# Two attention cores turn two key blocks into one tile, and the order of all instructions is computed with other costs

## The chip, the core and the metric

The kernel runs on one core of a Trainium2 chip. TensorE (PE) multiplies 128x128 blocks into PSUM; VectorE (DVE), ScalarE (ACT) and GpSimd (POOL) do the elementwise work; SyncE (SP) and ACT issue the transfers (DMA). The metric is the time of one execution on the device in microseconds (us), as a median of several.

## The reference

Two layers work on 512 latent tokens and 256 context tokens of width 1024. Each layer normalises and modulates its input, projects it to 4608 columns, runs three groups of attention heads beside a gate, and projects back. Cut to what matters here:

```python
def layer(x, cx, ...):
    hx = rmsnorm(x, norm_w) * (1 + scale[:, None, :]) + shift[:, None, :]
    px = split_cols(hx @ w_in)                       # the same for the context, hc and pc
    ya, yca = global_gqa(...)                        # A: every latent and context key
    yb, ycb = neighbourhood_attn(...)                # B: 8 x 16 window of keys, plus all context keys
    yc_, ycc = window_gqa(...)                       # C: keys within 128 tokens, plus all context keys, a sink
    ux = jnp.concatenate([ya, yb, yc_], axis=-1) * jax.nn.silu(px[9])
    x = x + gate[:, None, :] * (ux @ w_out)
```

`shift`, `scale` and `gate` come from `silu(c) @ ada_w + ada_b`. The context half is computed in the first layer alone. Everything is float32, and the output is the latent stream after a last RMSNorm.

## The kernel before

**Numbers in two parts.** Each operand of a large product is split into a high part (rounded to the matmul's float32r) and a low part, and three products (high-high, high-low, low-high) are added in PSUM. So a weight tile `ws` becomes `wh` (ACT, line 242) and `wl` (DVE or POOL, line 245), and a tile T of PSUM becomes `pth` (ACT) and `ptl` (DVE) in `pt_copy` (line 1019).

**Stages.** `body` first computes the modulation and the normalised, modulated input h. For each of 8 blocks of 128 features it loads two halves of an `ada` block (line 195), multiplies them (line 210), turns the result (line 218) and makes h (lines 394 to 400), from which the first matmuls of the projections (line 416) follow. The sums of squares of the input are added over the partitions by line 347 into `Obig`, raised to the power -1/2 on POOL (line 356), spread by line 364 into `Sbig`, and copied by ACT into `rb` (line 387). `mixers` then weaves the projections of the next head pair (lines 308 and 329) between the attention steps of the present one. The second half of the program's layer, p2, projects back (line 505) and prepares the next layer's h.

**One attention unit.** A unit is one head. `scores` multiplies query blocks with keys into `Sbig` (line 1028), DVE takes the row maximum, ACT the exponential into a tile P in SBUF, with queries on the partitions. The product with the values needs keys on the partitions, so P has to be turned block by block. `ship` (line 1030) has SP copy P into a tile R (`R5`, or `R2` for a smaller part) by DMA from SBUF to SBUF. `values` turns the 128x128 blocks of R for one key block into a PSUM tile T (`turn_r`, line 1042; shown as L1044), `pt_copy` brings T to SBUF, and `pv` multiplies it with the values into `Obig`. There are two tiles T, each one PSUM bank. `BandUnit` is group C, `NearUnit` group B, `GlobalUnit` group A; `CtxUnit` handles the context's queries. Key blocks 4 and 5 are the context, and all four query blocks use them. Of the latent key blocks, in C 0 and 3 are used by two query blocks each and 1 and 2 by three; in B all four are used by two. The loops take one key block per T, so a key block that two query blocks use fills 256 of T's 512 columns.

**What sets the order.** The loops only record instructions. `arrange` then computes the order in which each engine issues them: `Graph.run` goes through them as a list scheduler with costs per instruction, `Graph.back` gives ranks from the end, and the best of six rounds is fixed as the order of each engine. On the chip each engine issues in that order and waits for what an instruction needs; so the costs never become times, they only decide what stands ahead of what. The costs before: a DMA takes 2550 ns plus its bytes at 395 per ns, one after the other over all queues; a matmul that follows turnings costs 86 ns more; after a turning the next choice is a turning into the same tile T, if one is ready.

## Time and profile before

| | |
|---|---|
| median of 3 runs | 1173.37 us (1170.91, 1173.37, 1175.30) |
| the profiled execution, its own time | 1171.95 us |
| its span, first to last instruction | 1170.2 us |
| instructions in the span | 22714 |
| mean granted clock of PE | 0.995 |
| DMA | 191.41 MB, 164 GB/s on average |
| copies of P into R | 216 of 256 KB, 64 of 128 KB, 32 of 64 KB |

The page gives busy time per engine, the chain of work that ended last, and the costliest groups of instructions by line, with their mean duration and with the idle time of the engine ahead of them. Matmuls overlap in PE's pipeline, so their durations (about 0.28 us for 256 columns) are longer than the step from one start to the next; prices of PE's work are therefore read from the starts in the list of instructions in order of time. In that list a piece is: start, length, engine, line, operation, out<-in, shapes, count.

### The profile page before, as it was taken

How to read it: one execution, taken by the hardware profiler on the slowest of the kernel's cores; microseconds unless marked ns; L12 is line 12 of the kernel's file. 1: busy time of each engine (PE TensorE's matmuls, PEld its weight loads, DVE VectorE, ACT ScalarE, POOL GpSimd, SP SyncE). 2: the span in 40 equal slices, each digit the busy share in tenths (PEclk: the TensorE clock that was granted, in tenths of full speed). 3: DMA queues.
4: the chain of work that ended last, by engine and by line, in shares of the span. 5: the costliest groups of instructions: out<-in, count | busy, mean ns of one | idle time of the engine just before them, and what ended most of it. 6: DMA issues, size and time to landing. Idle time of an engine off the chain costs nothing.

```text
span 1170.2 us, 22714 instructions
## 1 busy us (share of the span) xinstructions
PE 1130.1 (97%) x8016; PEld 1015.5 (87%) x8016; DVE 765.4 (65%) x1548; ACT 696.4 (60%) x1581; POOL 406.7 (35%) x496
## 2 busy tenths in 40 slices
PE   5999999999999999999899999999999999999996
PEld 3799999998798897988787999988998989898886
DVE  6657676666456566666879765668674666667653
ACT  5546655565557567677742543555566777778651
POOL 2431212135446346357400021222234575667001
PEclk9999999999999999999999999999999999999999
DMA  9545434425444445435758542554243454556352
GB/s 350 196 131 177 152 123 160 147 102 169 146 154 156 155 149 192 156 131 182 251 188 304 175 138 83 172 176 139 103 160 122 156 169 149 172 180 216 118 172 72
DMA packets 105761, 191.41 MB, mean 164 GB/s; under 512 B 12208, under 2 KB 30768, under 8 KB 105648
## 3 DMA queue, kind: packets, MB, share of 16 engines
q1 hardware_dynamic: 101616, 181.71, 46.5%
q10 hardware_dynamic: 4032, 8.26, 1.9%
q8 instruction: 63, 1.03, 0.4%
q14 instruction: 50, 0.41, 0.1%
HBM read 109.05 MB, written 11.14 MB: 103 GB/s over the span
## 4 chain that ended last, share of the span: by engine, by line
PE 81%; DMA 6%; DVE 6%; ACT 4%; issue 2%; POOL 1%; SPq 0%; DVEq 0%; ACTq 0%; POOLq 0%
PE pj L329 18%; PE pj L308 18%; PE Obig L1028 9%; PE Sbig L1028 9%; PE T L1044 6%; PE pj L505 5%; DMA R<-P 4%; PE T L505 3%; PE Sbig L505 3%; PE T L329 2%; PE Sbig L416 1%; PE T L1047 1%; PE Sbig L329 1%; DVE junk L151 1%; PE pj L416 1%
## 5 line engine op out<-in xcount | busy, mean ns | idle before, releaser
L1024 DVE TENSOR_TENSOR ptl<-T,pth 128x512 fp32r<-128x512 f32 (+2 forms) x312 | 181.9, 592 | 98.4 <-ACT pth L778 93.8
L778 ACT ACTIVATE pth<-T 128x512 fp32r<-128x512 f32 (+2 forms) x312 | 159.2, 521 | 87.5 <-PE T L1044 75.9
L329 PE MATMUL pj<-wh,hL 128*128 128x256 f32 x896 | 184.4, 287 | 0.6 <-DVE kt L906 0.4
L308 PE MATMUL pj<-hL,wh 128*128 128x512 f32 x544 | 183.2, 401 | 0.3 <-DVE qt L894 0.2
L242 ACT ACTIVATE wh<-ws 128x512 fp32r<-128x512 f32 x192 | 120.0, 631 | 86.6 <-PE pj L308 25.1
L1028 PE MATMUL Sbig<-kt,qt 128*128 128x256 f32 (+1 forms) x864 | 155.7, 306 | 0.5 <-ACT P L1119 0.3
L329 PEld LDWEIGHTS pj<-wh,hL 128*128 128x128 f32 x896 | 145.7, 190 | 2.0 <-issue 0.7
L1044 PEld LDWEIGHTS T<-identr,R 128*128 128x128 f32 x1024 | 112.9, 141 | 33.0 <-DMA R<-P 9.4
L245 POOL TENSOR_TENSOR wl<-ws,wh 128x512 fp32r<-128x512 f32 x76 | 98.7, 1306 | 120.2 <-ACT wh L242 102.9
L1044 PE MATMUL T<-identr,R 128*128 128x128 f32 x1024 | 126.7, 239 | 10.2 <-DMA R<-P 6.7
L1028 PEld LDWEIGHTS Sbig<-kt,qt 128*128 128x128 f32 x864 | 125.1, 189 | 9.7 <-ACT P L1119 1.1
L1028 PE MATMUL Obig<-pth,vt 128*128 128x256 f32 (+2 forms) x432 | 128.7, 308 | 0.3 <-ACT pth L778 0.3
L1028 PE MATMUL Obig<-ptl,vt 128*128 128x256 f32 (+2 forms) x432 | 128.6, 312 | 0.2 <-DVE ptl L1024 0.2
L329 PE MATMUL pj<-wl,hL 128*128 128x256 f32 x448 | 128.0, 286 | 0.0
L245 DVE TENSOR_TENSOR wl<-ws,wh 128x512 fp32r<-128x512 f32 x116 | 82.5, 719 | 48.3 <-ACT wh L242 38.0
L308 PEld LDWEIGHTS pj<-hL,wh 128*128 128x128 f32 x544 | 98.3, 189 | 15.7 <-issue 0.4
L308 PE MATMUL pj<-hL,wl 128*128 128x512 f32 x272 | 109.2, 401 | 0.1
L1028 PEld LDWEIGHTS Obig<-pth,vt 128*128 128x128 f32 x432 | 81.4, 188 | 7.0 <-issue 1.5
L1150 DVE TENSOR_REDUCE negm<-Sbig 128x1 f32<-128x768 f32 x64 | 61.1, 955 | 38.4 <-PE Sbig L1028 22.4
L329 PEld LDWEIGHTS pj<-wl,hL 128*128 128x128 f32 x448 | 85.1, 190 | 0.4
L1028 PEld LDWEIGHTS Obig<-ptl,vt 128*128 128x128 f32 x432 | 81.5, 189 | 4.4 <-issue 0.9
L356 POOL TENSOR_TENSOR rstd<-rstd,mhalf 128x2 f32<-128x2 f32 (+1 forms) x6 | 5.4, 902 | 200.6 <-DVE rstd L354 200.6
(336 smaller groups left out, 2535.1 us busy)
## 6 DMA issues: line engine op xcount, KB each, us to landing
R<-P SPq DMA_DIRECT2D x216, 256.0 KB, 2.4
ws<-wf_dram SPq DMA_DIRECT2D x72, 256.0 KB, 3.3
ws<-wt_dram SPq DMA_DIRECT2D x72, 256.0 KB, 3.1
ada<-adaw_dram SPq DMA_DIRECT2D x32, 512.0 KB, 5.6
ws<-wo_dram SPq DMA_DIRECT2D x57, 256.0 KB, 3.4
bm<-mskB_dram SPq DMA_DIRECT2D x16, 576.0 KB, 4.2
R<-P SPq DMA_DIRECT2D x64, 128.0 KB, 2.2
dots<-adat_dram SPq DMA_DIRECT2D x16, 256.0 KB, 3.3
```

The lines of the kernel that those rows point to most:

```text
L151: return nc.vector.tensor_tensor_reduce(out=junk, in0=w, in1=row, op0=OP.mult, op1=OP.add, scale=1.0, scalar=m if half else sm[:, c:c + 1] ...
L242: nc.scalar.activation(hi, src, AF.Copy)
L245: eng.tensor_sub(lo, src, hi.bitcast(F32))
L308: nc.tensor.matmul(p[:, 0:n], a[:, r, :], cols(b[kt], c0, n), start=(i == 0), stop=(i == 23))
L329: nc.tensor.matmul(p[:, t * 256:(t + 1) * 256], tok(a[kt], t2 + t), b[:, r, :], start=(i == 0), stop=(i == 23))
L416: mm = nc.tensor.matmul(out, a, b, start=begin, stop=(kt == KT - 1 and i == 2), skip_group_check=True)
L505: nc.tensor.matmul(p[:, 0:n], a[:, r, :], ucols(ua[b][ft], c0, n), start=(ft == FT_ORDER[0] and i == 0), stop=(ft == FT_ORDER[-1] and i == 2))
L778: nc.scalar.activation(out, src, AF.Copy)
L1024: nc.vector.tensor_sub(lo[:, 0:n], T[:, 0:n], hi[:, 0:n].bitcast(F32))
L1028: return nc.tensor.matmul(*args, **kw)
L1044: return nc.tensor.transpose(out.bitcast(F32R), src, identr)
L1150: nc.vector.tensor_reduce(nm, S, axis=AX.X, op=OP.max, negate=True)
```

## The change

It has two parts. First, `values` of groups C and B puts two small key blocks into one tile T: 0 and 3 in C, 1 with 3 and 2 with 0 in B. The turnings and the products stay as many as they were, of the same widths; 96 copies of 256 columns by `pt_copy` (each by ACT and DVE) become 48 of 512. Which key block begins and which ends the accumulation in `Obig` is now named by its number.

Second, the planner's costs change. A DMA now has a fixed part and a rate by its source: 2400 ns and 340 bytes per ns from DRAM ("far"), 1650 and 395 from SBUF; transfers follow each other per issuing queue, overlap between queues costs half its length, and 700 ns pass to the landing. PE's steps count double before 21 us, a third turning in a row costs 20 ns more, float32 products are priced by shape. And after a turning, when none for the same T is ready, a turning into any tile that can be opened is now taken.

```diff
 class BandUnit(Unit):
         def values(self):
             O = psO()
-            for n, kb in enumerate((4, 5, 0, 1, 2, 3)):
-                qs = [i for i in range(4) if kb in self.pos[i]]
+            for kbs in ((4,), (5,), (0, 3), (1,), (2,)):
                 T = psT()
-                for j, i in enumerate(qs):
+                jobs = [(kb, [i for i in range(4) if kb in self.pos[i]]) for kb in kbs]
+                for j, (kb, i) in enumerate((kb, i) for kb, qs in jobs for i in qs):
                     o = self.pos[i][kb]
                     turn_r(T[:, j * 128:(j + 1) * 128], self.P[i], o)
-                k = len(qs) * 128
+                k = 128 * sum(len(qs) for _, qs in jobs)
                 pt = pt_copy(T, k)
                 yield k / 1200
-                pv(O, self.v(kb), pt, 0, qs[0] * 128, k, n == 0, n == 5)
+                o = 0
+                for kb, qs in jobs:
+                    pv(O, self.v(kb), pt, o, qs[0] * 128, len(qs) * 128, kb == 4, kb == 2)
+                    o += len(qs) * 128
                 yield k / 1200
...
 class NearUnit(Unit):
-            for n, kb in enumerate((4, 5, 1, 2, 3, 0)):
+            for kbs in ((4,), (5,), (1, 3), (2, 0)):
...
-TO_PE, TO_OTHER, FIXED, RATE = 400.0, 150.0, 2550.0, 395.0
+TO_PE, TO_OTHER, TO_LAND = 400.0, 150.0, 700.0
+SLOW = 21000.0
...
-            self.move = 3460.0 if stem(outs[0][0].name) == "bc" else b / RATE
+            far = any(u[0].name not in tiles or tiles[u[0].name][1] for u in ins)
+            self.fixed = 2400.0 if far else 1650.0
+            self.move = 3460.0 if out == "bc" else b / (340.0 if far else 395.0)
...
-            self.busy = (108.0 if n == 128 else 230.0) if exact else n / 2.4 + (13.5 if n > 128 else 12.0)
+            self.busy = {128: 108.0, 256: 57.0, 2: 112.0}[n] if exact else n / 2.4 + (13.5 if n > 128 else 12.0)
...
                 same = [x for x in now[e] if steps[x[1]].turn == prev.turn]
+                if not same:
+                    same = [x for x in now[e] if steps[x[1]].turn and all(
+                        slots[self.tag[z]] and self.place[z] == opened[self.tag[z]] for z in self.opens[x[1]])]
...
-                pipe = fin = max(t + FIXED, pipe) + s.move
+                begin = max(t + s.fixed, ring.get(e, 0.0))
+                fin = begin + s.move
+                for x, (a, b) in data.items():
+                    if x != e:
+                        fin += 0.5 * max(0.0, min(b, fin) - max(a, begin))
+                ring[e], data[e] = fin, (fin - s.move, fin)
                 lanes.append(fin)
+                fin += TO_LAND
...
+                row = row + 1 if s.turn else 0
+                if row > 2 and s.switch > 5:
+                    busy += 20
+                if t < SLOW:
+                    busy *= 2
+                    fin += s.last
```

Such costs move instructions all over the program. Three places matter for what follows.

The beginning of PE's order, before: the sums of squares (L347) stand in three pieces between the products with `ada` (L210).

```order
L347 MATMUL Obig<-ones,sq 128x2 x2
L210 MATMUL T<-ada,silu_c 2x256 x4
L347 MATMUL Obig<-ones,sq 128x2
L210 MATMUL T<-ada,silu_c 2x256 x4
L347 MATMUL Obig<-ones,sq 128x2
L210 MATMUL T<-ada,silu_c 2x256 x4
L218 MATMUL T<-ident,adasb 128x128 x2
L210 MATMUL T<-ada,silu_c 2x256 x4
L139 MATMUL T<-ident,silu_c 128x128 x4
L364 MATMUL Sbig<-ident,rstd 128x128 x4
```

And now:

```order
L347 MATMUL Obig<-ones,sq 128x2 x4
L210 MATMUL T<-ada,silu_c 2x256 x8
L364 MATMUL Sbig<-ident,rstd 128x128 x4
L218 MATMUL T<-ident,adasb 128x128 x2
L210 MATMUL T<-ada,silu_c 2x256 x3
L347 MATMUL Obig<-ones,sq 128x2 x2
L210 MATMUL T<-ada,silu_c 2x256
L139 MATMUL T<-ident,silu_c 128x128 x4
L210 MATMUL T<-ada,silu_c 2x256 x4
L364 MATMUL Sbig<-ident,rstd 128x128 x2
L416 MATMUL pj<-hL,wh 128x512 x2
```

All four sums for the latent tokens stand first, and the spreading of their result (L364) has moved ahead of the turnings L218 and L139.

PE in the first unit of group B that turns all its blocks, before (T and R with their numbers: R5_1608, 1530, 1563 and 1636 are the four query blocks): a matmul stands between the first two key blocks.

```order
L1044 MATMUL T_1638<-identr_77,R5_1608 128x128
L1044 MATMUL T_1638<-identr_77,R5_1530 128x128
L1044 MATMUL T_1638<-identr_77,R5_1563 128x128
L1044 MATMUL T_1638<-identr_77,R5_1636 128x128
L329 MATMUL pj_1707<-wh_1485,hC_625 128x256
L1044 MATMUL T_1683<-identr_77,R5_1608 128x128
L1044 MATMUL T_1683<-identr_77,R5_1530 128x128
L1044 MATMUL T_1683<-identr_77,R5_1563 128x128
L1044 MATMUL T_1683<-identr_77,R5_1636 128x128
```

And now, with the same unit's tiles under new numbers:

```order
L1044 MATMUL T_1618<-identr_77,R5_1588 128x128
L1044 MATMUL T_1618<-identr_77,R5_1510 128x128
L1044 MATMUL T_1618<-identr_77,R5_1543 128x128
L1044 MATMUL T_1618<-identr_77,R5_1616 128x128
L1044 MATMUL T_1663<-identr_77,R5_1588 128x128
L1044 MATMUL T_1663<-identr_77,R5_1510 128x128
L1044 MATMUL T_1663<-identr_77,R5_1543 128x128
L1044 MATMUL T_1663<-identr_77,R5_1616 128x128
L308 MATMUL pj_1792<-hL_241,wl_1783 128x512
```

The eight turnings stand in one row and fill both tiles T.

SP's queue where a unit of group A in the first layer copies its P into R, before:

```order
L251 DMA ws_4791<-wf_dram 128x512
L1039 DMA R5_4071<-P_4069 128x512
L1039 DMA R2_4072<-P_4069 128x256
L195 DMA ada_4057<-adaw_dram 128x1024
L251 DMA ws_4797<-wf_dram 128x512
L195 DMA ada_4059<-adaw_dram 128x1024
L1039 DMA R2_4079<-P_4076 128x256
L1039 DMA R5_4078<-P_4076 128x512
```

And now:

```order
L251 DMA ws_4701<-wf_dram 128x512
L195 DMA ada_3977<-adaw_dram 128x1024
L195 DMA ada_3979<-adaw_dram 128x1024
L251 DMA ws_4707<-wf_dram 128x512
L1039 DMA R5_3991<-P_3989 128x512
L1039 DMA R2_3992<-P_3989 128x256
L1039 DMA R2_3999<-P_3996 128x256
L1039 DMA R5_3998<-P_3996 128x512
```

Both halves of `ada` and the weight have moved ahead of the first pair of copies; before they stood between the two pairs.

More of the change, by code (lines that the diff above doesn't have):

```diff
@@ L1265, in values @@
             O = psO()
-            for n, kb in enumerate((4, 5, 1, 2, 3, 0)):
-                qs = [i for i in range(4) if kb in self.PLAN[i][4]]
+            for kbs in ((4,), (5,), (1, 3), (2, 0)):
                 T = psT()
-                for j, i in enumerate(qs):
+                jobs = [(kb, [i for i in range(4) if kb in self.PLAN[i][4]]) for kb in kbs]
+                for j, (kb, i) in enumerate((kb, i) for kb, qs in jobs for i in qs):
                     o = self.PLAN[i][4][kb]
                     turn_r(T[:, j * 128:(j + 1) * 128], self.P[i], o)
-                k = len(qs) * 128
+                k = 128 * sum(len(qs) for _, qs in jobs)
                 pt = pt_copy(T, k)
                 yield k / 1200
-                out = O[:, qs[0] * 128:qs[0] * 128 + k] if kb else O.rearrange("p (t c) -> p t c", t=4)[:, 0:4:3]
-                pv(out, self.v(kb), pt, 0, None, k, n == 0, n == 5)
+                o = 0
+                for kb, qs in jobs:
+                    n = len(qs) * 128
+                    out = O[:, qs[0] * 128:qs[0] * 128 + n] if kb else O.rearrange("p (t c) -> p t c", t=4)[:, 0:4:3]
+                    pv(out, self.v(kb), pt, o, None, n, kb == 4, kb == 0)
+                    o += n
                 yield k / 1200
@@ L1584, with __init__ @@
 class Step:
-    def __init__(self, inst):
+    def __init__(self, inst, tiles):
         self.inst, self.name = inst, inst.name
@@ L1598, in __init__, with cost @@
                                      str(a.dtype).split(".")[-1]))
-        self.cost()
-    def cost(self):
+        self.cost(tiles)
+    def cost(self, tiles):
         ins = [u for u in self.use if not u[1]]
@@ L1610, in cost @@
             b = 4 * outs[0][2][0][1] * size(outs[0][2])
-            self.busy = ISSUE.get(stem(outs[0][0].name).split("_")[0], 430.0)
-            self.move = 3460.0 if stem(outs[0][0].name) == "bc" else b / RATE
+            out = stem(outs[0][0].name).split("_")[0]
+            far = any(u[0].name not in tiles or tiles[u[0].name][1] for u in ins)
+            self.busy = ISSUE.get(out, 430.0)
+            self.fixed = 2400.0 if far else 1650.0
+            self.move = 3460.0 if out == "bc" else b / (340.0 if far else 395.0)
         elif e == "PE":
@@ L1748, in run @@
                 stage_left[self.pool[t]] += len(v)
-        lanes, pipe = [], 0.0
-        prev, done = None, 0
+        lanes, ring, data = [], {}, {}
+        prev, row, done = None, 0, 0
         def push(k):
@@ L1892, in arrange @@
 def arrange(tc, nc, needed):
-    steps = [Step(i) for i in nc.cur_bb.bb.instructions
+    tiles = {t.name: (t.tag, "DRAM" in str(t.space)) for t in tc.tiles}
+    steps = [Step(i, tiles) for i in nc.cur_bb.bb.instructions
              if type(i).__name__ not in ("BassTilePoolBoundary", "InstRegisterMove")]
-    tiles = {t.name: (t.tag, "DRAM" in str(t.space)) for t in tc.tiles}
     graph = Graph(steps, tiles, needed)
```

## The prediction, as made before the change was run

> **What bounds the kernel now.** I read the page's busy shares first, then the chain of waits, then the busy time by stage.
>
> ```profile
> PE 1130.1 (97%) x8016; PEld 1015.5 (87%) x8016; DVE 765.4 (65%) x1548; ACT 696.4 (60%) x1581; POOL 406.7 (35%) x496
> ...
> PE 81%; DMA 6%; DVE 6%; ACT 4%; issue 2%; POOL 1%; SPq 0%; DVEq 0%; ACTq 0%; POOLq 0%
> ```
>
> TensorE (PE) is busy for 1130.1 of 1170.2 us and holds 81% of the chain that ended last. DVE and ACT have a third of their time free. So the time is the sum of PE's instructions plus 40.1 us in which PE stands still. A change can win in two ways: cheaper PE instructions, or less standing still. Where PE stands still shows in the busy time by stretch (columns: stretch, its length, then busy us and instructions of PE, weight loads, DVE, ACT, POOL, the granted clock, DMA share, GB/s):
>
> ```profile
> 11.33:22.00 10.67, 9.71 (x73) 4.65 (x73) 5.55 (x22) 6.00 (x16) 1.14 (x1) 1.00 1.04 392
> 22.00:50.00 28.00, 26.89 (x215) 20.91 (x213) 19.44 (x46) 15.51 (x37) 13.50 (x11) 1.00 0.84 304
> 50.00:300.00 250.00, 248.69 (x1871) 231.76 (x1871) 165.16 (x354) 143.42 (x348) 67.80 (x94) 1.00 0.42 139
> 300.00:322.00 22.00, 19.67 (x129) 16.41 (x128) 10.52 (x19) 12.20 (x26) 11.39 (x11) 0.92 0.54 167
> 322.00:560.00 238.00, 234.02 (x1773) 209.53 (x1772) 150.04 (x303) 160.12 (x380) 126.09 (x154) 1.00 0.47 160
> 560.00:650.00 90.00, 83.49 (x439) 68.91 (x438) 76.82 (x150) 38.89 (x80) 9.04 (x6) 0.98 0.72 243
> 650.00:1120.00 470.00, 467.10 (x3309) 428.36 (x3308) 310.47 (x607) 296.31 (x661) 172.18 (x208) 1.00 0.45 150
> ```
>
> From 50 to 1120 us PE is idle for 17 us (1.3 + 2.3 + 4.0 + 6.5 + 2.9). The other 23 us are the head, up to 50 us, and the end. What ended the idle time of PE (us in total, times, longest):
>
> ```profile
> PE Obig L347 <- DVE sq L343: 11.3, 1, 11.3
> PE T L1044 <- DMA R<-P: 6.7, 7, 2.3
> PE T L1044 <- DVE ptl L1024: 3.0, 5, 1.8
> ```
>
> In the middle, turnings wait for the copy of P into R (6.7 us) and for a PSUM tile T still being read (3.0 us). A long stand has a second price, read from the granted clock:
>
> ```profile
> 317.90:321.30 3.40, 3.40 (x16) 2.91 (x15) 1.61 (x3) 2.18 (x7) 0.63 (x2) 0.50 0.00 0
> 380.00:384.00 4.00, 2.27 (x18) 1.62 (x18) 1.64 (x4) 1.78 (x6) 3.28 (x3) 1.00 0.87 283
> ...
> 573.90:577.30 3.40, 3.40 (x12) 2.62 (x12) 3.40 (x9) 2.14 (x4) 0.00 (x0) 0.50 0.74 230
> ```
>
> Right after the 2.3 us wait before 317.9 the clock was 0.50 for 3.4 us: 1.7 us of work lost. The same follows at 573.9. The 1.7 us stand within 380 to 384 cost no clock. So a stand over about 2 us costs 1.7 us more. (The Trainium skill, "TensorE: Matmul & The Clock Gate", Part 1, says the clock falls after at least one idle window of about 3.4 us; by that, neither stand should have cost clock and a removed stand would save its own length alone. This trace disagrees, and I go by it.)
>
> **Part 1: turnings in longer rows.** The order of PE's instructions keeps all 1024 turnings of R. Counted over the whole of PE's order, they stood in 315 unbroken rows (84 of two, 28 of three, 176 of four, 8 of five or six, 19 of eight) and now stand in 228 (none of two, 30 of three, 130 of four, 2 of seven, 66 of eight). Price of a row, from PE in order of time:
>
> ```profile
> 117.53 0.46 PE L1044 MATMUL T<-identr,R 128*128 128x128 f32 x4
> 117.83 0.35 PE L329 MATMUL pj<-wl,hL 128*128 128x256 f32 x1
> 118.02 0.40 PE L329 MATMUL pj<-wh,hL 128*128 128x256 f32 x2
> 118.25 0.28 PE L329 MATMUL pj<-wl,hL 128*128 128x256 f32 x1
> ...
> 123.78 0.28 PE L1044 MATMUL T<-identr,R 128*128 128x128 f32 x2
> 123.90 0.35 PE L329 MATMUL pj<-wh,hL 128*128 128x256 f32 x1
> 124.09 0.28 PE L1028 MATMUL Obig<-ptl,vt 128*128 128x256 f32 x1
> ...
> 183.01 0.79 PE L1044 MATMUL T<-identr,R 128*128 128x128 f32 x8
> 183.64 0.35 PE L308 MATMUL pj<-hC,wl 128*128 128x256 f32 x1
> 183.83 0.40 PE L308 MATMUL pj<-hC,wh 128*128 128x256 f32 x2
> ```
>
> Two matmuls of 256 columns step by 0.23 us (118.02 to 118.25), so one is 0.12. From a row's start to the start of the second matmul behind it, less one such step, a row of four costs 118.02 − 117.53 − 0.12 = 0.37, a row of two 124.09 − 123.78 − 0.12 = 0.19, a row of eight 183.83 − 183.01 − 0.12 = 0.70. The matmul behind a row starts its successor 0.07 late (0.19 instead of 0.12), which is what a longer row saves; but turnings from the third on are slower, so two rows of four (0.74) become 0.70 and no more. With three at 0.28 and five, six, seven between (0.45, 0.53, 0.62): before 16.0 + 7.8 + 65.1 + 3.9 + 13.3 = 106.1 us, now 8.4 + 48.1 + 1.2 + 46.2 = 103.9. **Saved: 2.2 us**, all on PE. Bounds: 1 us, if the longest rows run as slowly as four-rows end to end, and 6 us, if each of the 87 rows less saved a whole 0.07.
>
> **Part 2: small key blocks share a tile.** 96 pairs of copies of 256 columns become 48 of 512.
>
> ```profile
> L778 ACT ACTIVATE pth<-T 128x512 fp32r<-128x512 f32 x184 | 107.7, 598 | 49.4 <-PE T L1044 42.0 <-PE Obig L1028 5.4 <-DVE ptl L1024 0.4
> ...
> L778 ACT ACTIVATE pth<-T 128x256 fp32r<-128x256 f32 x96 | 36.7, 384 | 28.6 <-PE T L1044 26.2 <-PE Obig L1028 1.5
> ...
> L1024 DVE TENSOR_TENSOR ptl<-T,pth 128x512 fp32r<-128x512 f32 x184 | 124.9, 687 | 67.6 <-ACT pth L778 64.6 <-PE Obig L1028 1.3
> ```
>
> ACT saves 96 × 0.384 − 48 × 0.598 = 8.2 us, and DVE about as much by the same pairing. Neither sets the end, so this is worth nothing directly; the matmuls into Obig keep number and width. What it can give is earlier-free T tiles. A tile T is free after ACT's 0.60 and DVE's 0.69, 1.3 us, and the hand-overs between the engines; so I count reuses of a T bank that come with under 1.8 us of other PE work since its last turning. In the order before these are 50 of 412, now 23 of 364. (I added up PE's steps, 0.12 for 256 columns and 0.23 for 512, along each order.) Half the short reuses are gone, so I take half of the 3.0 us wait: **1.5 us**; bounds 0 and 3.0.
>
> **Part 3: the beginning.** PE in order of time before:
>
> ```profile
> 11.33 1.02 PE L347 MATMUL Obig<-ones,sq 128*128 128x2 f32 x4 [11.33 <-DVE sq L343]
> ...
> 14.72 0.59 PE L347 MATMUL Obig<-ones,sq 128*128 128x2 f32 x2
> 15.24 1.03 PE L210 MATMUL T<-ada,silu_c 128*2 128x256 f32 x8
> ...
> 15.59 1.14 POOL L356 TENSOR_TENSOR rstd<-rstd,mhalf 128x4 f32<-128x4 f32 x1 [14.30 <-DVE rstd L354]
> ...
> 18.17 0.60 PE L364 MATMUL Sbig<-ident,rstd 128*128 128x128 f32 x4
> ...
> 19.61 0.59 ACT L387 ACTIVATE rb<-Sbig 128x512 f32<-128x512 f32 x1
> ...
> 21.04 0.72 ACT L395 ACTIVATE hL<-x,mod 128x512 fp32r<-128x512 f32 x1 [0.32 <-DVE x L394]
> ...
> 21.97 0.49 PE L416 MATMUL pj<-hL,wh 128*128 128x512 f32 x1
> ```
>
> The sums of squares (L347) stood between groups of L210; now all four stand first, so they end near 13.2 instead of 15.3, the power on POOL near 14.9 instead of 16.7, and L364 follows 8 L210 (two groups, until about 15.2) instead of standing at 18.17. The broadcast `rb` then waits on ACT for the context squares, whose loads SP now issues ahead of the third half of `ada`; I put it near 16.5 instead of 19.61. `hL` would follow at about 18.2 and the first L416 2.9 us earlier. But ahead of it now stand L210, L347, L139 and the second L364, which needs DVE and POOL once more: 18.1 for the first x, 0.3 + 1.14 for the power, so L416 near 20.1. **Saved: 1.8 us**; bounds 0 (the `ada` loads, 392 GB/s at a DMA share of 1.04, set the pace instead) and 2.9. From 22 to 50 us PE is busy 26.89 of 28 us, so the earlier start is carried on and not lost in a wait.
>
> **Part 4: the order of the rest.** SP's queue moves loads against the copies R. Two of the chain's pieces are the late copies, the page's row of issues has the usual one:
>
> ```profile
> 311.05 6.55 DMA R<-P
> ...
> 378.40 5.35 DMA R<-P
> ...
> R<-P SPq DMA_DIRECT2D x216, 256.0 KB, 2.4
> ```
>
> In the first, both halves of an `ada` job and a weight stood ahead of the second pair of copies in SP's queue; now they stand ahead of both pairs (SP's rows in the part on the change). In the second, nothing stood ahead on SP, but ACT had issued a store of `u` just before:
>
> ```profile
> 378.32 0.33 ACTq L1358 DMA_DIRECT2D u<-u  x1
> ```
>
> The new planner counts half of such an overlap between queues; whether it moved this store clear, the order does not tell. Adding up PE's steps between the last score matmul of a block and its first turning: the least is 6.0 us before and 5.7 now, under 8 us 23 copies before and 22 now. So copies are no better covered than they were. I take **1 us** saved (the second place's wait, partly); bounds: 10 saved (all 6.7 and both losses of clock) and 8 lost (two more stands of 2.3 + 1.7).
>
> From the last sums of squares (L633) to the end every engine has the same order as before: nothing.
>
> **The sum** against the profiled execution's own 1171.95 us: − 2.2 − 1.5 − 1.8 − 1.0 = 1165.4 us. The median of the runs, 1173.37, lies 1.4 above that execution and its runs reach from 1170.91 to 1175.3. I put the change at 6.5 us and the time at **1166 us**, between 1165.4 and 1173.4 − 6.5 = 1166.9; own range 1161 to 1171.
>
> **Rivals.** *No change to be told* (about 0.5%, 6 us, is what a measurement of this kernel can tell from no change). Rows and head give 4.0 us, and the waits come back elsewhere, since copies are as tightly covered as before: 1173.4 − 4 + 2 = 1171 us. For it: the unchanged distances in part 4. Against it: fewer short reuses of T.
>
> *More than I say*: both losses of clock go with their stands. Then 6.7 + 3.4 + 3.0 + 2.2 + 1.8 = 17 us: 1156 us. Against it: late copies came from the queue ahead of them, and the queue is as full.
>
> *Slower, by late copies*: at each of the eight late `ada` jobs of the first layer SP now may have both halves ahead of all copies of a unit, as at the first place above. A stand there costs 2.3 + 1.7 = 4.0 us. From two more on, the 6.5 us are gone; with four more: 1173.4 − 6.5 + 16 = 1183 us, with three 1179.
>
> *Slower, by full banks*: a row of eight fills both T tiles, and PE cannot turn again until one is copied. There are 47 more such rows; 0.14 us of waiting at each eats the 6.5 us, 0.35 us gives 1173.4 − 6.5 + 16.5 = 1183 us. Against it: the 19 rows of eight before, as at 183.01, run straight on into matmuls, and reuses with little work between are fewer now. (The Trainium skill, "Perfetto Trace Analysis", section Matmuls, wants independent groups to rotate through PSUM banks so that one is emptied while the next is filled; filling both at once goes against it.)
>
> **How the numbers follow.** Forecast 0.50, no change 0.22, more 0.13, late copies 0.10, full banks 0.05. Against 1173.4, faster by over 0.5% means under 1167.5. I give that 0.8 of the forecast (0.40), all of "more", and a little of no change: 0.55. Slower takes most of the last two: 0.12. The rest, 0.33, is the same. The range from 1157 to 1176 leaves out half of "more" and the worse half of the slower cases.
>
> **What would show it.** L1044 in 228 rows with steps as priced; PE's wait on `ptl` near 1.5 us and on R near 6; the first L416 near 20 us; PE's busy time near 1126 and the copies of 256 columns gone. I am wrong in part 1 if rows of eight cost over 0.74; in part 3 if L416 stays at 22 or PE idles more from 22 to 50; in part 4 if the granted clock shows more than two dips before the end.

## The result and the profile after

| | before | changed |
|---|---|---|
| median | 1173.09 us (4 runs, 1170.91 to 1175.30) | 1156.69 us (4 runs, 1152.87 to 1158.13) |
| ratio to before, 95% interval | | 0.9855 [0.9825, 0.9885] |
| profiled execution, span | 1170.2 us | 1154.3 us |

The change saves 16.4 us. 1166 was forecast; 1156.7 lies 0.3 us below the range's low end. The rival "more than I say" had 1156. The page of the changed kernel:

```profile
PE 1122.4 (97%) x8016; PEld 1011.9 (88%) x8016; DVE 763.6 (66%) x1500; ACT 685.9 (59%) x1533; POOL 405.9 (35%) x496
```

PE is still the bound, with 7.7 us less busy time; some 32 us of standing are left of 40. Its waits (us in total, times, longest):

```profile
PE Obig L347 <- DVE sq L343: 11.2, 1, 11.2
PE T L1044 <- DVE ptl L1024: 2.4, 5, 0.7
...
PE T L505 <- ACT kept L242: 1.4, 1, 1.4
...
PE T L1044 <- DMA R<-P: 0.2, 1, 0.2
```

The wait on R has fallen from 6.7 to 0.2 us. The same stretches as before, with their columns:

```profile
11.33:22.00 10.67, 10.30 (x56) 5.18 (x56) 5.81 (x20) 5.46 (x14) 2.25 (x2) 1.00 1.03 387
22.00:50.00 28.00, 28.00 (x215) 18.98 (x216) 16.59 (x45) 14.05 (x36) 13.13 (x11) 1.00 0.70 262
50.00:300.00 250.00, 248.26 (x1879) 231.42 (x1879) 170.58 (x341) 141.05 (x330) 67.13 (x94) 1.00 0.44 144
300.00:322.00 22.00, 21.82 (x156) 18.68 (x155) 10.49 (x20) 13.43 (x28) 11.62 (x11) 1.00 0.51 168
322.00:560.00 238.00, 236.59 (x1822) 215.82 (x1821) 158.38 (x318) 166.38 (x397) 130.31 (x158) 1.00 0.51 173
560.00:650.00 90.00, 86.33 (x478) 73.61 (x479) 75.97 (x140) 35.76 (x68) 4.40 (x3) 1.00 0.72 244
650.00:1120.00 470.00, 466.18 (x3274) 426.24 (x3274) 309.50 (x585) 296.20 (x642) 171.49 (x207) 1.00 0.46 151
```

No stretch of the middle is at less than full clock: both losses (0.92 in 300 to 322, 0.98 in 560 to 650) are gone. (The clock's first record is its rise at the start, at 24.97 us here and 17.53 before; ahead of that the column prints 1.00 without a record.) By the starts of the same stages in both traces, the beginning up to the last L416 is 2.25 us slower (70.35 against 68.10), the first layer's attention (until its last projection, 548.69 and 540.80) 10.1 us shorter, the stage from there to the second layer's first projection (682.50 and 667.57) 7.0, the second layer's attention 0.4 longer, and the rest 1.3 shorter: 15.9 together.

**Where it came from**, by the two traces:

- rows of turnings: about 2.4 us of PE steps. In the list by time, a row of eight and what follows:

```profile
103.80 0.79 PE L1044 MATMUL T<-identr,R 128*128 128x128 f32 x8
104.43 0.47 PE L308 MATMUL pj<-hL,wh 128*128 128x512 f32 x1
104.74 0.40 PE L308 MATMUL pj<-hL,wl 128*128 128x512 f32 x1
```

  104.74 − 103.80 − 0.23 (a step of 512 columns) = 0.71, against 0.70 taken.
- the wait on R: 6.5 us, and the two losses of clock: 3.4 us. The first stood behind a wait on R (2.3 us, until 317.64), the second behind a wait for a tile T still being read (1.8 us, until 572.85).
- the second layer's products with `ada` on PE: 3.6 us, which the prediction did not count. They stand between 275 and 515 us, eight jobs of eight products. Before (first fence) and after (second), the job near 308 us; each product is two records:

```profile
307.45 1.04 PE L210 MATMUL pj<-ada,silu_c 128*2 128x256 f32 x14
308.42 0.53 PE L1044 MATMUL T<-identr,R 128*128 128x128 f32 x4
308.88 0.59 PE L210 MATMUL pj<-ada,silu_c 128*2 128x256 f32 x2
309.41 0.73 PE L308 MATMUL pj<-hL,wh 128*128 128x512 f32 x2
```

```profile
308.89 1.04 PE L210 MATMUL pj<-ada,silu_c 128*2 128x256 f32 x16
309.86 0.50 PE L308 MATMUL pj<-hL,wh 128*128 128x512 f32 x1
```

  From the start of a piece to the next start, eight products in one piece take 0.97 us, seven and one in two pieces 0.97 + 0.53 = 1.50. Before there were 18 pieces with 12.57 us in all, now 11 with 8.95. What a piece costs goes by fours: in all runs but d1, pieces of one to four products take 0.52 to 0.55 us (but for one of 0.69), pieces of five to eight 0.95 to 0.98. The products write by fours to four places, 32 rows of the PSUM tile apart, and in the trace the records of such a four start 7 ns apart, with 0.21 us from one four of records to the next. So it matters where a job is cut: seven and one cost 0.5 us more than eight, four and four 0.1. The changed kernel has such a piece of four:

```profile
499.81 0.61 PE L210 MATMUL pj<-ada,silu_c 128*2 128x256 f32 x8
500.35 0.39 PE L1028 MATMUL Obig<-pth,vt 128*128 128x256 f32 x1
```

- the beginning: 2.3 us lost. Some 2.3 us remain that I did not take apart. They are not waits: behind the last L416, PE is idle for 20.4 us instead of 26.6, and the 6.2 us less are no more than the wait on R fell by. They lie in PE's busy time, which fell by 11.9 us there, where rows, `ada` and clock give 9.4.

The late copies themselves are still there. In the changed kernel, the place where the prediction showed 6.55 us (SP's issues, then the summary of the copies issued from 310 to 320 us, then PE):

```profile
308.53 0.53 SPq L251 DMA_DIRECT2D ws<-wf_dram  x1
309.56 0.81 SPq L195 DMA_DIRECT2D ada<-adaw_dram  x2
310.46 0.38 SPq L251 DMA_DIRECT2D ws<-wf_dram  x1
310.94 3.79 SPq L1039 DMA_DIRECT2D R<-P  x4
```

```profile
DMA to landing us min/median/max: 2.5/5.6/6.1
```

```profile
316.89 0.52 PE L1028 MATMUL Sbig<-kt,qt 128*128 128x256 f32 x3
...
318.78 0.28 PE L308 MATMUL pj<-hC,wh 128*128 128x256 f32 x1
318.90 0.65 PE L1044 MATMUL T<-identr,R 128*128 128x128 f32 x3
```

Both `ada` halves and two weights stand ahead of all four copies, which land up to 6.1 us after their issue, as the rival "late copies" said. But the first turning of these tiles comes at 318.90, behind the projections of hC, and hardly waits; before it was due at 315.3 and stood until 317.64. The planner's own reckoning shows why: the old one had 4.6 us from issue to landing for the first late copy and the turning 0.5 us behind the landing (6.55 on the chip); the new one has 6.2 for the first of the four (6.13 on the chip) and puts the first turnings 0.3 to 1.6 us behind the landings.

### The profile page after: what moved, and what is told of

Same layout as the page of the kernel before. It is cut to its first block, busy times and chain, and to the rows that moved or that the text cites. A ratio compares the mean times of both kernels' runs of the same rounds, so it can differ in the third digit from the quotient of the medians.

```text
span 1154.3 us, 22566 instructions
## 1 busy us (share of the span) xinstructions
PE 1122.4 (97%) x8016; PEld 1011.9 (88%) x8016; DVE 763.6 (66%) x1500; ACT 685.9 (59%) x1533; POOL 405.9 (35%) x496
## 3 DMA queue, kind: packets, MB, share of 16 engines
q8 instruction: 63, 1.03, 0.4%
## 5 line engine op out<-in xcount | busy, mean ns | idle before, releaser
L1024 DVE TENSOR_TENSOR ptl<-T,pth 128x512 fp32r<-128x512 f32 (+1 forms) x264 | 172.5, 670 | 93.0 <-ACT pth L778 89.5
L778 ACT ACTIVATE pth<-T 128x512 fp32r<-128x512 f32 (+1 forms) x264 | 148.4, 585 | 69.8 <-PE T L1044 65.1
L329 PE MATMUL pj<-wh,hL 128*128 128x256 f32 x896 | 179.7, 285 | 0.8 <-DVE kt L906 0.8
L308 PE MATMUL pj<-hL,wh 128*128 128x512 f32 x544 | 180.2, 398 | 0.3 <-DVE qt L894 0.2
L1028 PEld LDWEIGHTS Sbig<-kt,qt 128*128 128x128 f32 x864 | 125.5, 189 | 10.7 <-DVE negm L1260 2.9
L1028 PE MATMUL Obig<-ptl,vt 128*128 128x256 f32 (+2 forms) x432 | 125.7, 308 | 1.1 <-DVE ptl L1024 1.1
L1044 PEld LDWEIGHTS T<-identr,R 128*128 128x128 f32 x1024 | 105.5, 140 | 20.4 <-DVE ptl L1024 6.6
L1044 PE MATMUL T<-identr,R 128*128 128x128 f32 x1024 | 115.3, 242 | 3.4 <-DVE ptl L1024 2.4
L245 DVE TENSOR_TENSOR wl<-ws,wh 128x512 fp32r<-128x512 f32 x116 | 85.2, 746 | 45.5 <-ACT wh L242 31.0
L308 PEld LDWEIGHTS pj<-hL,wh 128*128 128x128 f32 x544 | 97.7, 188 | 16.4 <-issue 0.9
```

The lines of the kernel that those rows point to most:

```text
L245: eng.tensor_sub(lo, src, hi.bitcast(F32))
L308: nc.tensor.matmul(p[:, 0:n], a[:, r, :], cols(b[kt], c0, n), start=(i == 0), stop=(i == 23))
L329: nc.tensor.matmul(p[:, t * 256:(t + 1) * 256], tok(a[kt], t2 + t), b[:, r, :], start=(i == 0), stop=(i == 23))
L778: nc.scalar.activation(out, src, AF.Copy)
L1024: nc.vector.tensor_sub(lo[:, 0:n], T[:, 0:n], hi[:, 0:n].bitcast(F32))
L1028: return nc.tensor.matmul(*args, **kw)
```

## The experiments

Three theories at the start. **Landing**: the transfers' costs by source place turnings late enough; that is the gain. **Tiles**: the shared tiles T are the gain, by rows and by tiles that come free earlier. **Any order**: each new order draws its own stands, and this one was lucky. All results in one table: median; ratio to before with its 95% interval; rows of turnings; pieces of the second layer's `ada` products and their time on PE; PE's wait on R and the stretches of half clock, both from 50 to 1120 us of the profiled run. (The rows hold 1152 turnings: the 1024 of R and 128 of tiles `qd`, which the prediction's count of rows took in too.) A profile is one execution, and some lie off their median: n2's took 1173.91 us, 6.1 more, n3's 1165.43, 3.8 more, d4's 1168.45, 2.7 less.

| kernel | median us | ratio | rows | ada pieces, us | wait on R | half clock |
|---|---|---|---|---|---|---|
| before | 1173.1 | 1 | 315 | 18, 12.57 | 6.7 | 2 |
| changed | 1156.7 | 0.9855 [0.9825, 0.9885] | 228 | 11, 8.95 | 0.2 | 0 |
| e1_values | 1171.1 | 0.9972 [0.9955, 0.9988] | 273 | 13, 10.39 | 9.2 | 1 |
| e2_planner | 1165.6 | 0.9936 [0.9923, 0.9949] | 271 | 15, 10.61 | 0.8 | 1 |
| e3_old_dma | 1156.9 | 0.9856 [0.9841, 0.9870] | 231 | 9, 8.32 | 3.8 | 0 |
| e4_no_rowrule | 1160.1 | 0.9885 [0.9868, 0.9901] | 270 | 13, 9.98 | 2.5 | 1 |
| n1_before_round5 | 1178.3 | 1.0039 [1.0021, 1.0057] | 313 | 17, 12.05 | 7.6 | 0 |
| n2_before_nudge | 1167.8 | 0.9955 [0.9939, 0.9971] | 322 | 15, 11.01 | 8.5 | 3 |
| n3_after_round6 | 1161.6 | 0.9885 [0.9862, 0.9908] | 229 | 13, 9.98 | 0.8 | 1 |
| n4_after_nudge | 1158.0 | 0.9867 [0.9842, 0.9891] | 223 | 12, 9.46 | 4.0 | 0 |
| c1_before_fp32 | 1169.4 | 0.9968 [0.9953, 0.9984] | 315 | 14, 10.50 | 4.0 | 1 |
| c2_after_old_fp32 | 1161.5 | 0.9900 [0.9878, 0.9922] | 226 | 19, 13.09 | 1.9 | 0 |
| c3_after_no_third | 1156.9 | 0.9854 [0.9831, 0.9878] | 236 | 10, 8.43 | 3.8 | 1 |
| c4_after_no_slow | 1155.5 | 0.9846 [0.9823, 0.9870] | 228 | 11, 8.95 | 0.9 | 0 |
| d1_before_long_ada | 1184.3 | 1.0083 [1.0070, 1.0097] | 315 | 18, 28.98 | 4.5 | 1 |
| d2_after_long_copies | 1160.2 | 0.9879 [0.9861, 0.9896] | 228 | 11, 8.95 | 0.8 | 0 |
| d3_after_ada122 | 1164.0 | 0.9912 [0.9899, 0.9926] | 228 | 17, 11.64 | 2.0 | 0 |
| d4_before_dma | 1171.2 | 0.9976 [0.9965, 0.9987] | 322 | 22, 14.41 | 1.5 | 0 |
| f1_before_whole_ada | 1177.7 | 1.0036 [1.0023, 1.0049] | 314 | 10, 8.84 | 9.0 | 2 |
| f2_after_whole_ada | 1156.4 | 0.9842 [0.9823, 0.9862] | 228 | 8, 7.80 | 3.2 | 0 |

### One part at a time

e1: the kernel before with the changed `values`. e2: the changed kernel with the old `values`. e3: the changed kernel with

```diff
-                begin = max(t + s.fixed, ring.get(e, 0.0))
-                fin = begin + s.move
-                for x, (a, b) in data.items(): ...
-                fin += TO_LAND
+                fin = max(t + 2550.0, ring.get(0, 0.0)) + s.move
+                ring[0] = fin
```

and `b / 395.0` for all sources. e4: the changed kernel without the lines `if not same: same = [...]`.

> The kernel before with the shared tiles alone (`values` of groups B and C as changed; the planner's costs and its row rule as before). PE's order has 273 rows of turnings (32 of three, 218 of four, 23 of eight) in place of 315; by the row prices PE's steps add up to 1.2 us less than before. Theory 'landing': the gain came from the planner's costs of transfers, so here nothing of it is seen: 1170 to 1173 us, PE's wait on R 5 us or more and at least one stretch of half clock in the middle. Theory 'tiles': the gain came from tiles T freed earlier, so here most of it is seen: 1158 to 1162 us. Theory 'any order': each new order of the rest draws its own waits on R; here any time from 1156 to 1178, with nothing in the edit that tells which.

> The changed kernel without the shared tiles (`values` as before; planner's costs and row rule as changed). 271 rows of turnings (68 of two, 28 of three, 112 of four, 10 of six, 53 of eight); by the row prices 1.6 us less than before. Theory 'landing': 1157 to 1160 us, wait on R under 2 us, no stretch of half clock in the middle. Theory 'tiles': 1168 to 1172 us. Theory 'any order': any time from 1156 to 1178.

> The changed kernel, but the planner has the transfers' costs of before (2550 ns and 395 bytes per ns for each, one after the other over all queues). 231 rows of turnings, PE's steps 0.1 us less than in the changed kernel. Theory 'landing': the wait on R is back (5 us or more, with one or two stretches of half clock): 1166 to 1170 us. Theory 'tiles': no change from the changed kernel, 1155 to 1159 us. Theory 'any order': any time from 1155 to 1172.

> The changed kernel without the rule that, when no turning for the same T is ready, any turning into a tile that can be opened is taken. 270 rows of turnings (32 of three, 212 of four, 26 of eight); by the row prices 1.6 us more than the changed kernel. Theories 'landing' and 'tiles' both say 1157 to 1160 us, with the wait on R still under 2 us. Theory 'any order': any time from 1155 to 1174.

1171.1, 1165.6, 1156.9 and 1160.1 us. "Tiles" alone falls with e1, "landing" alone with e3: without the new transfer costs all the gain is kept, though PE waits 3.8 us on R there and 0.2 in the changed kernel. e2, at 1165.6, is what neither of the two had expected (1157 to 1160, 1168 to 1172). The row rule is worth 3.4 us here, 1.6 of them by the row prices; that is within the scatter of the next part. Neither half of the change brings the whole.

### How much an order scatters

```diff
 n1, before:   -    for _ in range(CFG["turns"]):
               +    for _ in range(5):
 n2, before:   -FIXED, RATE = ..., 2550.0, 395.0     +FIXED, RATE = ..., 2570.0, 395.0
 n3, changed:  -        if best is None or max(end) < best[0]:
               +        if True:
 n4, changed:  -TO_LAND = 700.0                      +TO_LAND = 720.0
```

> The kernel before in every cost and rule, but the planner stops after five of its six rounds and so fixes another order (the best of the first five). Theory 'any order' (each order draws its own stands): the time moves by several us from 1173, anywhere from 1160 to 1180. Theory 'system' (what the change corrects makes every order of the old planner late): 1170 to 1176 us, with the waits on R and the stretches of half clock in the same stages, 300 to 330 and 560 to 600 us.

> The kernel before, with 2570 in place of 2550 ns as the planner's fixed time of a transfer: a nudge without a meaning, which gives another order (322 rows of turnings). 'Any order': anywhere from 1160 to 1180 us. 'System': 1170 to 1176 us.

> The changed kernel, but the last of the planner's six rounds is fixed instead of the best one (229 rows of turnings). 'Any order': several us from 1157, anywhere from 1152 to 1170. 'System': 1155 to 1160 us.

> The changed kernel, with 720 in place of 700 ns as the planner's time to landing, a nudge without a meaning (223 rows of turnings). 'Any order': anywhere from 1152 to 1170 us. 'System': 1155 to 1160 us.

The kernel before takes 1167.8, 1173.1 and 1178.3 us in three orders, the changed one 1156.7, 1158.0 and 1161.6. So an edit without a meaning moves the time by up to 5 us ("any order" is right on that; n1 and n2 lie outside the 1170 to 1176 of "system"), but the two groups don't meet: their means are 1173.1 and 1158.8, and some 14 us belong to the change. It also means that a single order can't settle a part of 4 us; the comparisons below are read with that.

### Which cost

```diff
 c1, before:   -(108.0 if n == 128 else 230.0) if exact
               +{128: 108.0, 256: 57.0, 2: 112.0}[n] if exact
 c2, changed:  the same, the other way
 c3, changed:  -                if row > 2 and s.switch > 5:
               -                    busy += 20
 c4, changed:  -SLOW = 21000.0                       +SLOW = 0.0
```

> The kernel before with one cost changed: the planner's price of float32 products as in the changed kernel (57 ns for 256 columns, 112 for 2, where it had 230). 315 rows of turnings as before, so nothing from rows. Theory 'price of ada' (eight products with `ada` take PE 0.98 us on the chip, the old planner has 1.84 for them, so it counts on cover for the copies R that isn't there, at 317 and 382 us): stands in 300 to 550 us fall from 20 to 12 us or less, the time to 1161 to 1167 us. Theory 'third turning' (rows of turnings were priced too low): no change, 1168 to 1178 us. Theory 'head' (pricing PE double at the start shifts the rest): no change.

> The changed kernel with the old price of float32 products (230 ns for 256 and for 2 columns). 226 rows of turnings. 'Price of ada': the stands on R near 317 and 382 us are back, PE's wait on R 5 us or more, 1164 to 1172 us. 'Third turning' and 'head': 1155 to 1162 us.

> The changed kernel without the 20 ns that a third turning in a row costs more. 236 rows of turnings. 'Third turning': 1164 to 1172 us, with waits on R and T back. 'Price of ada' and 'head': 1155 to 1162 us.

> The changed kernel without the doubled price of PE before 21 us. The order of turnings is that of the changed kernel (228 rows); PE's order in the first 60 us is another. 'Head': 1164 us or more. 'Price of ada' and 'third turning': 1155 to 1162 us. On the beginning: if the late rise of the clock (24.97 us in the changed kernel, 17.53 before) comes from the new order of the head, it is back near 17.5 here and the time falls by 2 us, to 1153 to 1156; if it comes with the run, it stays.

The price of the third turning and the doubled price at the start are worth nothing that these runs can tell (1156.9 and 1155.5). The float32 price is worth 4.1 us in c1 against the runs of before beside it (I had expected 6 to 12) and 4.8 in c2. c2 missed too: "price of ada" wanted 1164 us or more and 5 us or more of waits on R; 1161.5 and 1.9 came, which is what the other two theories had said. Sorted by that price and by the tiles, the means over all orders that the planner made (without d3, whose price lies between) are

| | old `values` | shared tiles |
|---|---|---|
| price 230 | 1172.6 (before, n1, n2, d4) | 1166.3 (e1, c2) |
| price 57 | 1167.5 (c1, e2) | 1158.0 (changed, e3, e4, n3, n4, c3, c4) |

By these means the price is worth 5 to 8 us and the shared tiles 6 to 10. With orders that scatter by 5 us and only two orders in two of the cells these sizes are rough, and whether the two add up or help each other can't be told. Single orders overlap: c2's 1161.5 lies within the changed kernel's own orders (1155.5 to 1161.6), and n2's 1167.8 below c1's 1169.4; e1, e2 and d4 differ from their cells in other costs as well. That both count is what the means say together; no single run shows it.

### How the price acts, with the order held still

In d1 each of the second layer's first four products of a job is issued three times over, to the same place; in f1 the pieces of such a job are moved down to its last product. The repeated products don't enter the plan, each stands behind its original, and all else keeps before's order in both. f2 does in c4's order what f1 does.

```diff
 d1:  -                    nc.tensor.matmul(pm[...], ...)
      +                    a = [nc.tensor.matmul(pm[...], ...)
      +                         for _ in range(3 if n == 0 and k >= KT else 1)]
 f1:  +    for job in list(jobs.values())[8:]:
      +        at = pe.index(job[-1])
      +        for k in reversed(job[:-1]):
      +            if at - pe.index(k) <= 40:
      +                pe.remove(k)
      +                at = at - 1
      +                pe.insert(at, k)
```

> The kernel before, every engine's order kept as it was, but each of the second layer's eight `ada` jobs issues its first four products three times over (the same values into the same place), so that a job of 0.98 us takes PE some 1.8 us: what the old planner had counted for it. That is 8 x 0.86 = 6.9 us more work on PE between 275 and 515 us. Theory 'price of ada' (those jobs are cover for the copies R, and the old order counted on more of it): the stands on R near 317 and 382 us shrink, PE's wait on R falls under 4 us, and the time rises by 3 us or less, to 1172 to 1176. Theory 'any order' (the price only drew a better order): the waits stay and the time rises by 6 us or more, to 1179 to 1182.

The repeated products cost more than I had reckoned: PE's time for the jobs rose from 12.57 to 28.98 us, 16.4 more and not 6.9. The time rose by 10.2 us against the runs of before beside it. By these medians about 6 us were absorbed; in the two profiles the span grew by 13.3 us (1183.5 against 1170.2), and only 3.1 were. The stretch around the first late copy, before and in d1:

```profile
316.00:322.00 6.00, 4.36 (x22) 3.87 (x23) 2.24 (x5) 2.71 (x7) 1.33 (x4) 0.72 0.14 55
```

```profile
316.00:322.00 6.00, 5.49 (x37) 4.68 (x35) 2.85 (x6) 2.68 (x5) 2.50 (x2) 1.00 0.58 181
380.00:386.00 6.00, 6.00 (x59) 4.05 (x57) 3.87 (x8) 4.60 (x12) 5.10 (x5) 1.00 0.73 238
```

The loss of clock near 318 is gone (1.7 us), the stand near 383 too, and the wait on R is 4.5 instead of 6.7. My number for the time was missed, since the added work was more than twice what I had set: sixteen products in one piece took 3.13 us, where eight take 0.97. The cover is real, but only 3 to 6 of 16.4 us were absorbed.

> The kernel before, planned as before, but in PE's order the products of one of the second layer's `ada` jobs are moved down to stand directly ahead of the job's last one (where that is at most 40 places away); nothing else moves. 18 pieces become 10. In the traces a job in one piece takes 0.975 us and each further piece some 0.52 us more (18 pieces 12.57 us, 11 pieces 8.95). Theory 'pieces' (the old price cut the jobs into pieces, and that is part of what it cost): the pieces take 8.4 us instead of 12.6, and the time falls by 3 to 5 us, to 1169 to 1171 us. Without it, because PE then waits elsewhere: 1172 to 1176 us.

> The changed kernel without the doubled price at the start, and with the jobs of `ada` put together in the same way (11 pieces become 8). 'Pieces': 1.5 us less than without it, 1153 to 1155 us, the fastest of all; otherwise 1155 to 1158 us.

f1 did what the edit says (10 pieces, 8.84 us, 3.7 less) and became 4.1 us slower than the runs of before beside it, outside both expectations. Its waits:

```profile
PE T L1044 <- DMA R<-P: 9.0, 10, 2.1
PE T L1044 <- DVE ptl L1024: 4.1, 6, 1.8
```

R 9.0 instead of 6.7, T 4.1 instead of 3.0, and all PE waits from 50 to 1120 us 24.0 instead of 16.1. "Pieces" as a cause by itself falls: fewer pieces did not make this order faster. That a piece of `ada` taken from between turnings uncovers them is how I read the waits; d1 and f1 agree on it from both sides, each with one order. In f2 pieces fell by 1.15 us and the wait on R rose by 2.3; 1156.4 us, no change.

> The changed kernel with the price that the traces show for a product with `ada`, 122 ns (eight take 0.975 us), in place of 57, and without the doubled price of PE before 21 us. 228 rows of turnings. 'Price of ada' as a question of too much alone: as without the doubled price, 1154 to 1158 us. If a right price is better than a low one: 1150 to 1153 us. If what helps is a low price: 1159 us or more.

```diff
-            self.busy = {128: 108.0, 256: 57.0, 2: 112.0}[n] if exact ...
+            self.busy = {128: 108.0, 256: 122.0, 2: 112.0}[n] if exact ...      (and SLOW = 0.0)
```

1164.0 us: the right price, 122 ns, is 8.5 us worse than the low one (c4, also without the doubled price at the start). With 57 the planner counts on 0.46 us of cover for a job that gives 0.97, and what it leaves out is a reserve; with 122 there is none (17 pieces, wait on R 2.0). That reading fits d1 and f1, but it rests on one order at 122, and n1 and n2, with the same costs but for a nudge, lie 10.5 us apart: it is not shown. Nor does all of the difference lie where the copies are: in the profiles the last L416 starts at 72.85 us in d3 and at 67.98 in c4, 4.9 us that have nothing to do with R. And 122 is right only for a job in one piece; a single product in a piece of its own costs 0.52.

### The transfers' costs alone, and the copies' length

d4 puts the changed kernel's transfer costs into the kernel before. d2 keeps the changed kernel's order and copies the first 16 columns of each of the 48 shared tiles once more.

```diff
 d4:  -                pipe = fin = max(t + FIXED, pipe) + s.move
      +                begin = max(t + s.fixed, ring.get(e, 0.0))
      +                fin = begin + s.move      (overlap and 700 ns to landing as in the change)
 d2:  +            EXTRA[a.ins.name] = [nc.scalar.activation(hi[:, 0:16], T[:, 0:16], AF.Copy).ins]
      +            EXTRA[a.ins.name] = [nc.vector.tensor_sub(lo[:, 0:16], T[:, 0:16], hi[:, 0:16]...).ins]
```

> The kernel before with one cost changed: the transfers' (fixed time and rate by source, queues apart, 700 ns to landing) as in the changed kernel. 322 rows of turnings. Theory 'landing' in what is left of it (these costs help where the price of ada is still wrong): 1161 to 1167 us, PE's wait on R under 3 us. Without it: 1168 to 1178 us.

The wait on R in d4:

```profile
PE T L1044 <- DVE ptl L1024: 2.3, 5, 0.9
...
PE T L1044 <- DMA R<-P: 1.5, 3, 0.5
```

6.7 has become 1.5 us and no stretch of half clock is left, 8.6 us less, yet the time fell by only 2.9 (1171.2). Within that, `ada` came in 22 pieces (1.8 us more), and PE stands more for other things (10.7 us of waits beside R's, 9.4 before). The largest part of what was lost again lies in the beginning: in d4's profile the last L416 starts at 72.28 us instead of 68.10, 4.2 later, with a clock that rose only at 24.73. So "landing" is right on the wait and wrong on the time. Over all runs the planner made: with old transfer costs PE waits 3.8 to 9.2 us on R (before, e1, e3, n1, n2, c1), with new ones 0.2 to 4.0.

> The changed kernel, every engine's order kept as it is, but each of the 48 shared tiles T has its first 16 columns copied once more by ACT and by DVE behind the copy, some 0.17 us on each: about what the 96 small copies cost more than the 48 large ones. Theory 'copies' (the shared tiles gain because ACT and DVE have less to do per key block and T comes free earlier): 4 us or more of the gain go, 1160 to 1163 us. Theory 'order' (they gain by longer rows and by what the planner then can place): 1156 to 1158 us.

The added copies took, as wanted (columns as in the page's groups, mean ns of one behind the bar):

```profile
L1025 ACT ACTIVATE pth<-T 128x16 fp32r<-128x16 f32 x48 | 8.8, 183 | 1.5
L1028 DVE TENSOR_TENSOR ptl<-T,pth 128x16 fp32r<-128x16 f32 x48 | 8.4, 175 | 1.6
```

and the time rose to 1160.2 us, 3.5 by the medians, with ratios whose intervals overlap. In the profiles, the part behind the last L416 takes 1088.3 us instead of 1083.95, 4.4 more. The waits on T:

```profile
PE T L1048 <- DVE ptl L1028: 2.4, 4, 1.3
PE T L1048 <- DVE ptl L1026: 2.2, 5, 0.7
```

4.6 us instead of 2.4, half of it behind the added copies themselves. So about half of what the shared tiles gain fits shorter work of ACT and DVE per key block, though neither engine is busy for more than two thirds of the span. That is one pair of kernels, and its intervals overlap. Rows, at 2.4 us for the whole change, can be a part of the other half; the runs don't take it further apart.

## Why the prediction was right or wrong

**Direction right, size wrong; the step that failed is part 4.** It put 1 us on "the order of the rest", between 10 saved and 8 lost. Measured: the wait on R fell by 6.5 us and both losses of clock (3.4) went, 9.9 together, the bound of 10; and 3.6 us of `ada` pieces had no row in the sum at all, so they were put at nothing without a reason. The reason given was that the least PE work between a unit's last scores and its first turning was 6.0 before and 5.7 now, and that as many copies had under 8 us. Both are true and told nothing: the two long stands on R were at copies that land 6.55 and 5.35 us after issue, and those have their own distance. For the late pair at 311.05 it was 9.1 us of PE steps before, and 10.5 now. I read the least of all distances where the distance of the late ones was the question.

**Part 1** held: 228 rows, about 2.4 us against 2.2, 0.71 us for a row of eight against 0.70. It speaks of 1024 turnings, but its rows hold 1152, with 128 of the tiles `qd`, taken at the same prices.

**Part 2**: the copies of 256 columns are gone, but the wait on `ptl` fell from 3.0 to 2.4 and not to 1.5. The worth of the shorter copies was still more than the 1.5 put down if d2 is right, 3.5 to 4.4 us: without them waits on T rise by 2.2 us and smaller ones beside. "Off the path" was too easy for engines that hand PE its next tile.

**Part 3** failed: L416 first started at 22.05, as before, not at 20.1. The order alone is not the cause. d2 has the same order of every engine; the same rows of the changed kernel and of d2:

```profile
20.75 1.03 PE L210 MATMUL T<-ada,silu_c 128*2 128x256 f32 x8
21.71 0.69 PE L364 MATMUL Sbig<-ident,rstd 128*128 128x128 f32 x2
22.05 1.20 PE L416 MATMUL pj<-hL,wh 128*128 128x512 f32 x2
```

```profile
19.57 0.61 PE L210 MATMUL T<-ada,silu_c 128*2 128x256 f32 x8
20.12 0.43 PE L364 MATMUL Sbig<-ident,rstd 128*128 128x128 f32 x2
20.85 0.73 PE L416 MATMUL pj<-hL,wh 128*128 128x512 f32 x2 [0.30 <-ACT wh L242]
```

The same products take 1.03 us in the one and 0.61 in the other: PE ran at full clock from 24.97 us in the changed kernel's profile and from 17.78 in d2's (17.53 before). With the clock up as early as before, L416 comes 1.1 us earlier, but the last L416, with which that stage ends, starts at 68.04, before at 68.10: the head start is not "carried on". So the order of the head gives nothing, and the late clock cost 2.3 us in the one profile (70.35). c4, with another order of the head, was to tell the two apart; its clock rose at 18.89 us, as if the order were the cause, but in f2, with c4's head, at 25.35.

**The sum.** −2.2 −1.5 −1.8 −1.0 was forecast; measured by profile are −2.4 (rows), −9.9 (R and clock), −3.6 (`ada`), +2.3 (head), and about −2.3 in PE's busy time that I did not take apart, −15.9. The rival "more than I say" named the mechanism of the largest part and came within 1 us, partly by chance: its 3.0 for `ptl` and 1.8 for the head did not come, and `ada` stood in for them. I had held against it that the queue is as full as before. It is, and the copies are as late; what moved is when PE asks for them.

**The rivals against.** "Late copies" was right on SP's queue (all four copies behind both halves) and wrong on the price, for the same reason. "Full banks" fell: 47 more rows of eight, and the wait of turnings on `ptl` is lower, not higher.

**The price of a stand** was wrong as a rule ("a stand over about 2 us costs 1.7 us more"). The lengths between two changes of the granted clock are whole multiples of 3.413 us in all traces (before: 88 of them up to 317.90, 1 at half clock, 74, 1, 172). In the middle of the program what counts is the idle time inside one such stretch. In n4_after_nudge a stand of 2.6 us at 571.4 lies across a border, and the clock stays; in n2_before_nudge two stands of 0.9 and 0.7 us lie in one stretch, and the next runs at half clock:

```profile
569.47:572.88 3.41, 1.89 (x11) 1.36 (x10) 3.41 (x9) 2.22 (x6) 0.00 (x0) 1.00 0.93 326
572.88:576.30 3.42, 2.27 (x15) 1.96 (x16) 2.33 (x7) 2.29 (x7) 0.00 (x0) 1.00 0.73 242
576.30:579.71 3.41, 3.41 (x23) 2.71 (x22) 2.53 (x7) 0.98 (x2) 0.00 (x0) 1.00 0.51 166
```

```profile
315.02:318.44 3.42, 1.79 (x12) 1.38 (x11) 0.46 (x2) 0.60 (x1) 1.63 (x1) 1.00 0.46 172
318.44:321.85 3.41, 3.41 (x19) 3.22 (x18) 2.60 (x5) 2.11 (x6) 0.91 (x3) 0.50 0.04 15
```

Counted over the 20 profiles from 40 to 1120 us, stretches of 3.413 us at full clock: 14 with 1.63 us or more of idle PE, each followed by one at half clock, and 6277 with 1.61 or less, none of them. (The Trainium skill, "TensorE: Matmul & The Clock Gate", Part 1, has windows of 3413 ns that run on regardless of the program, which agrees, and wants at least one idle window before the clock falls, which does not: not quite half of a window was enough.) The changed kernel's fullest stretch of idle stays below that. In the beginning this does not hold: in e3_old_dma the clock rose at 18.80 us and fell again after a stretch with 1.35 us of idle PE.

```profile
18.80:22.21 3.42, 2.07 (x18) 1.03 (x16) 3.19 (x6) 3.15 (x9) 0.00 (x0) 1.00 0.98 353
22.21:25.63 3.41, 3.35 (x21) 1.49 (x22) 2.84 (x10) 2.40 (x5) 1.05 (x2) 0.50 1.03 417
```

So the border near 1.62 us is one of this kernel's middle, and what exactly is counted as idle stays open.

## What to carry to other kernels

Where a scheduler's order decides, ask for each late transfer how much work stands between it and its use; the least distance over all transfers says nothing about the late ones. Cheap work of the bound engine that lies between a transfer and its use is cover: f1 took 3.7 us of it away and became 4.1 us slower, though one order is thin proof. Before crediting an edit of a scheduler's costs with a few us, time two or three nudges without a meaning: here they alone moved the kernel by up to 5 us.

## What the runs showed that I had not expected

- From 40 to 1120 us, the half clock follows a stretch of 3.413 us in which PE idles for 1.63 us or more, not a stand of some length (above). So whether a stand costs 1.7 us more depends on where its borders fall, which changes from run to run.
- PE's clock rises at the start at a time that the order alone does not set: in 20 profiles for the first time between 16.5 and 25.4 us after the span's start. Two pairs with the same order of the beginning differ by 7.2 us (24.97 and 17.78) and 6.5 us (25.4 and 18.9), and by 2.3 and 2.4 us at the end of that stage. What it waits for stays open: in the changed kernel PE was busy for 7.44 of the 7.44 us from 17.53 to 24.97.
- A piece of one to four float32 products of 256 columns with two rows, each to its own quarter of the rows, takes PE 0.52 to 0.55 us, a piece of five to eight 0.95 to 0.98. So the 0.12 us per product of a whole job is no price of a single one, and f1's "each further piece some 0.52 us more" is wrong for four and four (1.08 us in two pieces, 0.97 in one). Products issued again to the same place cost 0.26 us each (16.4 us for 64 of them).
- A price in a planner that is too low (57 ns for 122) gave a faster program than the one that fits a whole job, in one order at 122; that it acts as a reserve is argued, not shown.
- No version here is shown to beat the changed kernel: 0.9846 [0.9823, 0.9870] and 0.9842 [0.9823, 0.9862] overlap its 0.9855.
